# Value products a round later, the exponential's scale inside the minimum, and an early stage re-ordered

## The chip, the cores and the metric

The kernel runs on one NeuronCore of a Trainium2 chip. Five engines work from queues of their own and meet through semaphores: TensorE (PE in the profile, its weight loads PEld) multiplies matrices, VectorE (DVE) and ScalarE (ACT) do elementwise work and reductions, GpSimd (POOL) does smaller elementwise work, and SyncE (SP) issues the DMAs. The metric is the device time of one execution in microseconds (us).

## The reference

Two layers over a sequence of 2048 tokens of width 1024, each with eight input projections, two groups of heads and an output projection, and a residual around the whole. Cut to what matters:

```
hn = rms_norm(x, norm_gain)
aq, ak, av, ag, rq, rk, rv, rg = split(hn @ w_in)          # eight times 512 columns
# A: 8 heads of 64, chunks of 64 tokens, own chunk and 8 before it, learned bias by distance
p  = softmax(q k^T * 64**-0.5 + bias);  ya = p @ v
# B: 4 heads of 128, retention: decay by distance, rotary phases on q and k
t1*c - t2*s, t1*s + t2*c                                     # the rotation, halves of a head
yr = rms_norm(o_intra + o_inter)
y  = concat(ya * silu(ag), yr * silu(rg))
x  = x + y @ w_out
```

After the second layer comes a last RMSNorm. All in float32; the kernel keeps that precision by splitting each operand of a matmul into a high and a low half of 16 bits and adding three products (high by high, high by low, low by high).

## The kernel before

Activations lie transposed in `hTh` and `hTl` (high and low), in four blocks of 512 tokens for a layer. The loops run over layers `l`, over four groups of heads `s` (two attention heads and one retention head) and, inside, over the four token blocks `n`. For each (l, s, n) `dense_T` (L608) makes the four projections that are wanted transposed (attention q and k, retention q and k) as four PSUM tiles `dT` of 128 x 512, each with 24 matmuls of 512 columns (L731); `dense_V` (L738) makes the values and gates as four tiles `dV`, one for each 128 tokens, again 24 matmuls (L752). These tiles share two PSUM buffers (`psD`). ScalarE and VectorE evacuate them, in `evacuate` (L627) and, for `dV`, at L760 to L770.

The order of every engine but SP is written out by hand. `run` (L152) steps a dense generator, which yields after each third of a tile (8 matmuls): a *round*. In each round it fires what `later(k, fn)` (L595) had put off by k rounds, then steps the attention of the block before by one round, and then pulls some steps of background work (`push`, `pull`: weight preparation, norms, tables) so that it is spread over the rounds that are left. An engine works through its queue strictly in that order: an instruction that waits holds all that are behind it. SP's order is written out only for the first block, and is left to the scheduler after it.

`attention` (L778) handles eight units of a block (four tiles of 128 queries, `a`, by two heads, `hx`), three rounds each. In the first round it calls `flow(1)` (L588), which takes the oldest value product `pv` out of `pipe` if more than one is there, that of two units before; then `qk` puts the scores of this unit into PSUM tile `S` (L800, L801). VectorE adds the bias and takes the row maximum in one instruction (L804), makes the exponential's bias from it (L806), ScalarE takes the exponential (L807) and rounds it (L809), POOL makes the remainder (L810), and a transposing DMA on SP's queue (L812) brings both into `pT`, which has two buffers. `pv` multiplies `pT` by the values (L820 to L822) into a PSUM tile of its own for each head, from a ring of four (`psR`) that is shared with retention and with the column sums; `out_` (L824) takes the reciprocal of the row sum (L826), multiplies it by a scale (L827), and multiplies the head by it and by the gate (L832). Retention's products are made in `decayed` (L870) and `retention` (L884), in the units with hx = 1.

The rotation of retention's q and k (j = 2 and 3 in `evacuate`): ScalarE copies the tile to SBUF (L662), two DMAs swap the halves of the head (L666, L667), VectorE multiplies by cosine and sine tables and adds (L670), and the result is rounded and its remainder taken (L673, L676). The tables of a block come from `tables` (L83), some twenty small VectorE steps and two sines on ScalarE (L121, L122), stored to DRAM and loaded for each use (`tab_load`, L613).

Weights are loaded in sections of 128 columns; ScalarE sums their squares (`sumsq`, L305), VectorE casts the sum (`lowp`, L314), TensorE adds over partitions (`allsum`, L319), and the section is scaled by a power of two and split (`convert`). `prep_T` and `prep_V` do this for the next group, `prep_Omax` (L494) sums the squares of all of w_out.

The first block, (0, 0, 0), has an order of its own (the step list at L1363): its tokens are normalised and transposed tile by tile; tokens 512 to 1023 are normalised during its `dense_V`, one step of a list in each round (L1368), and `dense_T` of the second block needs them.

## Time and profile before

| | us |
|---|---|
| median of 3 runs | 2094.44 |
| lowest and highest | 2092.88, 2094.84 |
| the profiled execution | 2094.75 |
| its span | 2092.8 |

| engine | busy us | share of the span |
|---|---|---|
| PE | 2004.4 | 96% |
| VectorE | 1343.8 | 64% |
| ScalarE | 1141.3 | 55% |
| POOL | 432.9 | 21% |

The granted TensorE clock was 0.991 of full speed in the mean. A row of a group reads: line, engine, operation, tiles written and read, shapes, count, then busy time in us and the mean in ns of one instruction, then the idle time of the engine just ahead of them and what ended it. A row of waits reads: who waited for whom, total us, number of times, longest. A row of the timeline reads: start, duration, engine, line, instruction; in brackets the idle time ahead of it and what ended it.

### The profile page before, as it was taken

What the parts mean: (1) busy time and instruction counts of PE and PEld (TensorE: products, weight loads), DVE (VectorE), ACT (ScalarE), POOL (GpSimd) and SP (SyncE); (2) the same over time, 40 slices, a digit from 0 to 9 for tenths busy, and PEclk for the clock granted to TensorE, in tenths of its full rate; (3) what the DMA queues carried; (4) which work ended last, traced back from release to release, by engine and by line L of the source; (5) the groups of instructions that cost most, each with busy time, mean ns of one, the idle gap of its engine ahead of it and who ended that gap; (6) DMA issues with size and microseconds to landing.
All of it is one profiled execution on the core that took longest, in us unless ns stands there. A gap on an engine that the chain in (4) does not pass through costs nothing.

```text
span 2092.8 us, 39599 instructions
## 1 busy us (share of the span) xinstructions
PE 2004.4 (96%) x14014; PEld 1049.4 (50%) x14014; DVE 1343.8 (64%) x4031; ACT 1141.3 (55%) x2522; POOL 432.9 (21%) x509
## 2 busy tenths in 40 slices
PE   6888999999999999998999999999999999998998
PEld 4344455555555555444444555555555555554443
DVE  7676666666656666576654666666666667656643
ACT  7455665556565654455444546554655565455432
POOL 1022222222122212121000222222222222222100
PEclk9999999999999999999999999999999999999999
DMA  8767674557476764599965556655655776558874
GB/s 247 171 127 162 136 166 114 115 112 159 110 169 133 161 166 99 113 211 260 219 185 113 120 102 142 130 121 106 155 123 118 178 156 162 117 100 183 212 199 123
DMA packets 645702, 313.65 MB, mean 150 GB/s; under 512 B 459232, under 2 KB 602080, under 8 KB 645504
## 3 DMA queue, kind: packets, MB, share of 16 engines
q1 hardware_dynamic: 645504, 311.12, 66.4%
q8 instruction: 110, 1.80, 0.4%
q14 instruction: 88, 0.72, 0.1%
HBM read 123.26 MB, written 41.98 MB: 79 GB/s over the span
## 4 chain that ended last, share of the span: by engine, by line
PE 55%; DMA 7%; DVE 5%; ACT 3%; issue 1%; SPq 1%; POOL 0%; POOLq 0%; DVEq 0%; ACTq 0%
PE dT L731 18%; PE dV L752 15%; PE dO L1105 12%; DMA pT<-pq 2%; PE r L860 2%; PE S L801 2%; PE S L800 2%; PE o L820 1%; PE o L821 1%; PE o L822 1%; DVE sc L804 1%; DMA swp<-rot 1%; DMA yhy<-rhy 1%; ACT sc L807 1%; ACT pq L809 1%
## 5 line engine op out<-in xcount | busy, mean ns | idle before, releaser
L810 POOL TENSOR_TENSOR pq<-sc,pq 128x640 f16<-128x640 f32 (+4 forms) x256 | 323.8, 1265 | 1175.9 <-issue 590.7
L807 ACT ACTIVATE sc<-sc,mq,cT 128x640 f32<-128x640 f32 (+4 forms) x256 | 218.5, 853 | 558.1 <-DVE mq L806 413.7
L752 PE MATMUL dV<-whV,hTh 128*128 128x512 f16 x1024 | 354.5, 382 | 13.0 <-DVE gt L770 12.8
L731 PE MATMUL dT<-hTh,whT 128*128 128x512 f16 x1008 | 349.4, 382 | 14.7 <-DMA hTh<-hTl 9.6
L752 PE MATMUL dV<-wlV,hTh 128*128 128x512 f16 x1024 | 354.1, 381 | 0.0
L752 PE MATMUL dV<-whV,hTl 128*128 128x512 f16 x1024 | 354.0, 381 | 0.0
L731 PE MATMUL dT<-hTl,whT 128*128 128x512 f16 x1008 | 346.6, 379 | 0.0
L731 PE MATMUL dT<-hTh,wlT 128*128 128x512 f16 x1008 | 346.6, 379 | 0.0
L752 PEld LDWEIGHTS <-hTh 128*128 128x128 f16 x2048 | 197.3, 98 | 227.7 <-DVE gt L770 16.4
L731 PEld LDWEIGHTS <-whT 128*128 128x128 f16 x2016 | 192.9, 98 | 221.6 <-issue 24.1
L804 DVE CUSTOM_DVE_ANT_0 sc<-S,bias 128x640 f32<-128x640 f32 (+4 forms) x256 | 188.4, 736 | 78.8 <-PE S L801 61.1
L1105 PE MATMUL dO<-whO,yly 128*128 128x512 f16 x512 | 194.1, 379 | 2.4 <-DMA yly<-rly 2.4
L1105 PE MATMUL dO<-whO,yhy 128*128 128x512 f16 x512 | 194.0, 379 | 1.2 <-DVE gt L770 0.6
L1105 PE MATMUL dO<-wlO,yhy 128*128 128x512 f16 x512 | 194.0, 379 | 0.0
L809 ACT ACTIVATE pq<-sc 128x640 f16<-128x640 f32 (+4 forms) x256 | 171.5, 670 | 10.9 <-DMA pT<-pq 3.0
L1105 PEld LDWEIGHTS <-yhy 128*128 128x128 f16 x1024 | 99.6, 98 | 115.1 <-issue 0.8
L752 PEld LDWEIGHTS <-hTl 128*128 128x128 f16 x1024 | 99.7, 98 | 105.0 <-issue 2.8
L800 PE MATMUL S<-k,q 128*128 128x128 f16 (+3 forms) x592 | 143.1, 268 | 7.9 <-DVE mq L804 7.9
L731 PEld LDWEIGHTS <-wlT 128*128 128x128 f16 x1008 | 97.2, 98 | 101.8 <-issue 1.1
L820 PE MATMUL o<-v,pT 128*128 128x65 f16 x1120 | 129.6, 193 | 10.2 <-DMA pT<-pq 9.7
L801 PE MATMUL S<-k,q 128*128 128x128 f16 (+3 forms) x592 | 130.5, 268 | 0.0
L820 PEld LDWEIGHTS <-pT 128*128 128x128 f16 x1120 | 105.3, 97 | 49.2 <-DMA pT<-pq 21.3
(350 smaller groups left out, 3352.7 us busy)
## 6 DMA issues: line engine op xcount, KB each, us to landing
q<-qq SPq DMA_DIRECT2D x128, 128.0 KB, 2.7
yyy<-y_d SPq DMA_DIRECT2D x32, 512.0 KB, 4.6
stT<-in_w_in_dram SPq DMA_DIRECT2D x27, 512.0 KB, 4.8
stV<-in_w_in_dram SPq DMA_DIRECT2D x26, 512.0 KB, 4.5
k<-kk SPq DMA_DIRECT2D x128, 64.0 KB, 2.0
swp<-rot SPq DMA_DIRECT2D x64, 128.0 KB, 2.5
tabc<-tab SPq DMA_DIRECT2D x32, 256.0 KB, 2.7
tabs<-tab SPq DMA_DIRECT2D x32, 256.0 KB, 2.9
```

Of the source, the lines that this page charges most:

```text
L731: pe.matmul(ps, w_[:, j, kt, :], h_[:, kt, :], start=(m == 0), stop=(m == 23))
L752: pe.matmul(ps, h_[:, kt, a * P:(a + 1) * P], w_[:, kt, :], start=(m == 0), stop=(m == 23))
L800: pe.matmul(o, st.q[:, hx, 0, cs], k_, start=True, stop=False)
L801: pe.matmul(o, st.q[:, hx, 1, cs], k_, start=False, stop=True)
L804: dve.tensor_tensor_reduce(out=v, in0=S[:, 0:w], in1=g.bias[hx][:, 640 - w:640], scale=1.0, scalar=-3.0e38, op0=ALU.add, op1=ALU.max, accu ...
L807: act.activation(v, v, AF.Exp, bias=m[:, 0:1], scale=g.c[:, 0:1])
L809: act.activation(pq[:, 0:w], v, AF.Copy)
L810: pool.tensor_tensor(pq[:, w:2 * w], v, pq[:, 0:w], op=ALU.subtract)
L820: pe.matmul(o[:, 0:65], u.p[:, b, :], v_[:, 0:65], start=(b == 0), stop=False)
L821: pe.matmul(o[:, 0:64], u.p[:, b, :], v_[:, 65:129], start=False, stop=False)
L860: pe.matmul(out_, w_, m_, start=(i == 0), stop=(i + 1 == len(pairs)))
L1105: pe.matmul(ps, h_[:, kt, :], w_[:, kt, :], start=(m == 0), stop=(m == 23))
```

## The change

- `attention`: `flow(1)` is called after the unit's first round instead of ahead of its scores, so each value product stands one round later.
- `qk`: VectorE's instruction multiplies by the (negative) scale `g.nc`, read from a column, and takes the minimum; a POOL addition of one column replaces VectorE's L806, and the exponential's scale is -1.
- `pv` and `out_`: both heads of a query tile share one PSUM tile; after the second, one reciprocal and one multiplication serve two columns.
- `tables`: one round more ahead of the two sines, except for the first block.
- First block: the rotation reads the PSUM tile directly (VectorE multiplies by the sine with input and output on different halves of the partitions, in two instructions for a tile) instead of a ScalarE copy and two swap DMAs for each of the two tiles. Its first retention product is put 11 rounds after the start of its `dense_V` instead of into the attention.
- Second block: q and k of the attention are projected in eight pieces of 128 columns, with 24 matmuls each, in an order that takes the last 128 tokens last.
- Weight sums: the cast stands one round after ScalarE's sum of squares, in `prep_T` and `prep_V`; `prep_Omax` writes its eight sums into eight columns, reduces them once, loads two sections ahead, and is pushed one dense generator earlier with 22 steps.

```
@@ tables
         yield
+        if n:
+            yield
         act.activation(r, ang, AF.Sin)
         act.activation(k2, k, AF.Sin)
...
@@ Sections, prep_T
         def square(self, j):
             nm = f"{self.nm}{j}"
-            self.sq[j] = lowp(sumsq(self.sts[j], nm, self.g.h[:, j]), nm)
+            self.sq[j] = sumsq(self.sts[j], nm, self.g.h[:, j])
+
+        def cast(self, j):
+            self.sq[j] = lowp(self.sq[j], f"{self.nm}{j}")
...
             w.square(j)
             yield
+            w.cast(j)
             yield
...
@@ prep_Omax
+        load(0)
+        load(1)
+        yield
         for j in range(KT):
...
+            if j + 2 < KT:
+                load(j + 2)
+            yield
+            act.activation(st[j], st[j], AF.Square, accum_out=ms[:, j:j + 1])
+            yield
+        yield
+        m1 = b2.tile([P, 1], F32, tag="m1", name=f"m1{nm}", bufs=4)
+        dve.tensor_reduce(m1, ms, axis=AX.X, op=ALU.add)
+        mm = lowp(m1, nm)
+        for _ in range(2):
             yield
...
@@ dense_T
+        def first_rotation(j, ps, rot):
...
+            def cosine():
+                dve.scalar_tensor_tensor(out=own, in0=ps, scalar=2.0 ** -16, in1=st.tabc, op0=ALU.mult, op1=ALU.mult)
+
+            def sine(half):
...
+                i_, o_ = slice((1 - half) * 64, (2 - half) * 64), slice(half * 64, half * 64 + 64)
+                dve.scalar_tensor_tensor(out=st.swp[o_], in0=ps[i_], scalar=-2.0 ** -16, in1=st.tabs[i_], op0=ALU.mult,
+                                         op1=ALU.mult)
...
+            d = 2 * j
+            later(d, cosine)
+            later(d, lambda: sine(0))
+            later(d + 1, lambda: sine(1))
+            later(d + 2, lambda: dve.tensor_tensor(own, own, st.swp, op=ALU.add))
+            later(d + 3, lambda: act.activation(rot[:, 0], own, AF.Copy))
+            later(d + 4, lambda: dve.tensor_tensor(rot[:, 1], own, rot[:, 0], op=ALU.subtract))
...
+        parts = (l, s, n) == (0, 0, 1)
+        if parts:
+            ps, m = [None] * 2, 0
+            for (j, a) in ((0, 0), (0, 1), (0, 2), (1, 0), (1, 1), (1, 2), (0, 3), (1, 3)):
...
+                for i in range(24):
+                    w_, h_ = ((g.h, hh), (g.l, hh), (g.h, hl))[i // KT]
+                    pe.matmul(ps[j][:, cs], w_[:, j, i % KT, :], h_[:, i % KT, cs], start=(i == 0), stop=(i == 23))
...
@@ attention
-            dve.tensor_tensor_reduce(out=v, in0=S[:, 0:w], in1=g.bias[hx][:, 640 - w:640], scale=1.0, scalar=-3.0e38,
-                                     op0=ALU.add, op1=ALU.max, accum_out=m)
-            dve.tensor_scalar(m, m, g.nc[:, 0:1], LN_PSC, op0=ALU.mult, op1=ALU.add)
-            act.activation(v, v, AF.Exp, bias=m[:, 0:1], scale=g.c[:, 0:1])
+            dve.tensor_tensor_reduce(out=v, in0=S[:, 0:w], in1=g.bias[hx][:, 640 - w:640], scale=g.nc[:, 0:1],
+                                     scalar=3.0e38, op0=ALU.add, op1=ALU.min, accum_out=m)
+            pool.tensor_tensor(m, m, lnp, op=ALU.add)
+            act.activation(v, v, AF.Exp, bias=m[:, 0:1], scale=-1.0)
...
+                rl = b2.tile([P, 2], F32, tag="rl", name=f"rl{u.nm}")
+                dve.reciprocal(rl, o2[:, 0:2, 64])
+                dve.tensor_scalar(rl, rl, g.ka[:, 0:1], None, op0=ALU.mult)
...
         for i, (a, hx) in enumerate(units):
+            u = qk(a, hx)
+            yield
             flow(1)
-            u = qk(a, hx)
-            yield
...
-            elif a == 0 and (l, s, n) == (0, 0, 0):
-                decayed(l, s, n, g, st, 0)
...
@@ the loop over blocks
+                if n == 2 and s == 2:
+                    push(prep_Omax(l, go), 22)
...
-                if n == 2 and s == 2:
-                    push(prep_Omax(l, go), 13)
...
-                if (n, s) == (0, 0) and not first:
+                if (n, s) == (0, 0):
                     later(11, lambda n=n, g=g, st=st: decayed(l, s, n, g, st, 0))
```

More of the change, by code (lines that the diff above doesn't have):

```diff
@@ L62, in hybrid_trunk @@
     pool.memset(mhalf, -0.5)
+    lnp = cp.tile([P, 1], F32, tag="lnp", name="lnp")
+    pool.memset(lnp, LN_PSC)
     invf_sb = cp.tile([P, 1], F32, tag="invf", name="invf_sb")
@@ L134, in tables @@
         yield
-    TAB_STEPS = 19
+    TAB_STEPS = 20
     class St:
@@ L441, in prep_V @@
             yield
-            m1[j] = lowp(sq(j), f"{nm}{j}")
-            yield from rest(3)
+            m1[j] = sq(j)
+            yield
+            m1[j] = lowp(m1[j], f"{nm}{j}")
+            yield from rest(2)
             m = allsum(m1[j], f"{nm}{j}")
@@ L495, in prep_Omax, with load @@
         nm = f"O{l}"
-        mm = b2.tile([P, 1], F32, tag="omax", name=f"omax{nm}")
-        st = load_sec(w_out[l, :, 0:P], f"{nm}m0")
+        ms = b2.tile([P, KT], F32, tag="omax", name=f"omax{nm}", bufs=1)
+        st = []
+        def load(j):
+            t_ = w4.tile([P, KT, P], F32, tag="w4", name=f"st{nm}m{j}")
+            sp.dma_start(t_, w_out[l, :, j * P:(j + 1) * P].rearrange("(k p) c -> p k c", p=P))
+            st.append(t_)
+        load(0)
+        load(1)
+        yield
         for j in range(KT):
+            if j + 2 < KT:
+                load(j + 2)
             yield
-            m1 = sumsq(st, f"{nm}m{j}", None)
-            if j + 1 < KT:
-                st = load_sec(w_out[l, :, (j + 1) * P:(j + 2) * P], f"{nm}m{j + 1}")
-            if j == 0:
-                dve.tensor_copy(mm, m1)
-            else:
-                dve.tensor_tensor(mm, mm, m1, op=ALU.add)
-        mm = lowp(mm, nm)
-        for _ in range(4):
+            act.activation(st[j], st[j], AF.Square, accum_out=ms[:, j:j + 1])
[5 more added lines that the diff above has]
+        for _ in range(2):
             yield
@@ L625, in soon, with tokens @@
                 later(1, fn)
+        def first_rotation(j, ps, rot):
+            if j == 2:
+                st.rq = rot
+                later(1, tab_load)
+                own = rot[:, 1:3].rearrange("p a c -> p (a c)").bitcast(F32)
+            else:
+                st.rk = rot
+                own = b1.tile([P, 512], F32, tag="qq", name=f"raw{nm}")
+            st.swp = []
+            def cosine():
+                dve.scalar_tensor_tensor(out=own, in0=ps, scalar=2.0 ** -16, in1=st.tabc, op0=ALU.mult, op1=ALU.mult)
+            def sine(half):
+                if half == 0:
+                    st.swp = b1.tile([P, 512], F32, tag="swp", name=f"swp{nm}_{j}")
+                i_, o_ = slice((1 - half) * 64, (2 - half) * 64), slice(half * 64, half * 64 + 64)
+                dve.scalar_tensor_tensor(out=st.swp[o_], in0=ps[i_], scalar=-2.0 ** -16, in1=st.tabs[i_], op0=ALU.mult,
+                                         op1=ALU.mult)
+            def tokens():
+                st.kt = b1.tile([P, KT, P], F16, tag="ktok", name=f"kt{nm}")
+                sp.dma_start_transpose(out=st.kt, in_=rot.rearrange("p a c -> p (a c)"))
+            d = 2 * j
[5 more added lines that the diff above has]
+            later(d + 4, lambda: dve.tensor_tensor(rot[:, 1], own, rot[:, 0], op=ALU.subtract))
+            if j == 2:
+                later(d + 5, lambda: act.activation(rot[:, 2], rot[:, 0], AF.Copy, scale=2.0 ** -11))
+            else:
+                later(d + 6, tokens)
         def evacuate(j, ps):
@@ L657, in evacuate @@
                 rot = b2.tile([P, w, 512], F16, tag=f"rot{j}", name=f"rot{nm}_{j}")
+                if first:
+                    first_rotation(j, ps, rot)
+                    return
                 if j == 2:
@@ L683, in tokens @@
                         sp.dma_start_transpose(out=st.kt, in_=rot.rearrange("p a c -> p (a c)"))
-                    d = 5 if j == 2 and first else 3
+                    d = 3
                     later(d, turned(raw, raw, st.tabc, ALU.mult))
@@ L693, in swap @@
                     else:
-                        later(d + 5 if first else 11, tokens)
+                        later(11, tokens)
                 if j == 2:
@@ L698, in evacuate @@
                     swap()
-                    if first:
-                        later(1, tab_load)
                 else:
                     st.rk = rot
-                    later(8 if first else 2, swap)
+                    later(2, swap)
         if first:
@@ L717, in dense_T @@
                 yield
-        for j in range(2 if first else 0, 4):
+        parts = (l, s, n) == (0, 0, 1)
+        if parts:
+            ps, m = [None] * 2, 0
+            for (j, a) in ((0, 0), (0, 1), (0, 2), (1, 0), (1, 1), (1, 2), (0, 3), (1, 3)):
+                if a == 0:
+                    ps[j] = psD.tile([P, 512], F32, tag="dense", name=f"dT{nm}_{j}")
+                cs = slice(a * P, (a + 1) * P)
+                for i in range(24):
+                    w_, h_ = ((g.h, hh), (g.l, hh), (g.h, hl))[i // KT]
+                    pe.matmul(ps[j][:, cs], w_[:, j, i % KT, :], h_[:, i % KT, cs], start=(i == 0), stop=(i == 23))
+                    m += 1
+                    if m % 32 == 0 and m < 192:
+                        yield
+                if a == 3:
+                    evacuate(j, ps[j])
+            yield
+        for j in range(2 if first or parts else 0, 4):
             if j == 2 and not first:
@@ L782, in attention @@
                 units.append((a, hx))
-        ya = {}
         def qk(a, hx):
@@ L816, in pv @@
             t = 4 * n + u.a
-            o = psR.tile([P, 512], F32, tag="small", name=f"o{u.nm}")
+            if u.hx == 0:
+                ring["o"] = psR.tile([P, 4, P], F32, tag="small", name=f"o{u.nm}")
+            o2 = ring["o"]
+            o = o2[:, u.hx]
             for b, (q_, a_) in enumerate(u.kts):
@@ L822, in pv @@
                 pe.matmul(o[:, 0:65], u.p[:, u.nb + b, :], v_[:, 0:65], start=False, stop=(b == u.nb - 1))
+            if u.hx == 0:
+                return
             def out_():
-                rl = b2.tile([P, 1], F32, tag="rl", name=f"rl{u.nm}")
-                dve.reciprocal(rl, o[:, 64:65])
-                dve.tensor_tensor(rl, rl, g.ka, op=ALU.mult)
-                if u.hx == 0:
-                    ya[u.a] = b2.tile([P, P], F32, tag="ya", name=f"ya{u.nm}")
-                y = ya[u.a]
-                vs = slice(u.hx * 64, u.hx * 64 + 64)
-                dve.scalar_tensor_tensor(out=y[:, vs], in0=o[:, 0:64], scalar=rl[:, 0:1], in1=st.g[u.a][:, vs],
-                                         op0=ALU.mult, op1=ALU.mult)
-                if u.hx == 1:
-                    sp.dma_start(y_d[t][:, s * P:(s + 1) * P], y)
+                rl = b2.tile([P, 2], F32, tag="rl", name=f"rl{u.nm}")
+                dve.reciprocal(rl, o2[:, 0:2, 64])
+                dve.tensor_scalar(rl, rl, g.ka[:, 0:1], None, op0=ALU.mult)
+                y = b2.tile([P, P], F32, tag="ya", name=f"ya{u.nm}")
+                for hx in range(2):
+                    vs = slice(hx * 64, hx * 64 + 64)
+                    dve.scalar_tensor_tensor(out=y[:, vs], in0=o2[:, hx, 0:64], scalar=rl[:, hx:hx + 1],
+                                             in1=st.g[u.a][:, vs], op0=ALU.mult, op1=ALU.mult)
+                sp.dma_start(y_d[t][:, s * P:(s + 1) * P], y)
             later(1, out_)
@@ L840, in attention @@
         for i, (a, hx) in enumerate(units):
-            flow(1)
             u = qk(a, hx)
             yield
+            flow(1)
             if hx == 1:
```

## The prediction

> **What bounds the kernel now.** I read the page's first lines, then the table by stage, then TensorE's waits, then the timeline around the longest.

> ```profile
> span 2092.8 us, 39599 instructions
> PE 2004.4 (96%) x14014; PEld 1049.4 (50%) x14014; DVE 1343.8 (64%) x4031; ACT 1141.3 (55%) x2522; POOL 432.9 (21%) x509
> ```

> TensorE (PE) is the bound: 88 us of the span are left to it in which it does nothing. A change that adds and removes no matmul work can only win from those 88 us, and from matmuls run at a reduced clock. Where they lie, by stage (columns: stretch and its length, then busy time of PE, weight loads, VectorE, ScalarE and POOL, then granted clock, DMA share, GB/s):

> ```profile
> 69.00:205.00 136.00, 107.26 (x693) 54.11 (x692) 95.50 (x269) 72.69 (x154) 26.57 (x35) 0.92 0.71 150
> 205.00:860.00 655.00, 644.29 (x4793) 343.39 (x4793) 425.19 (x1378) 375.89 (x874) 157.18 (x176) 1.00 0.64 136
> 860.00:985.00 125.00, 112.13 (x767) 56.69 (x766) 82.29 (x231) 69.03 (x132) 24.82 (x26) 0.97 0.92 207
> 1090.00:1870.00 780.00, 776.06 (x5636) 411.04 (x5635) 503.42 (x1573) 435.00 (x1025) 180.36 (x204) 1.00 0.60 131
> ```

> The long steady stretches leave TensorE 11 us idle in 655 and 4 us in 780. The early stretch, 69 to 205 us, leaves 29 of 136 and runs at 0.92 of the clock; the hand-over between layers leaves 13 of 125, with the DMA engines 92% busy. What TensorE waits for:

> ```profile
> PE dV L752 <- DVE gt L770: 12.8, 6, 4.9
> PE o L820 <- DMA pT<-pq: 9.7, 11, 2.2
> PE dT L731 <- DMA hTh<-hTl: 9.6, 1, 9.6
> PE msT L323 <- DVE mbT L316: 3.3, 3, 1.9
> PE msV L323 <- DVE ya L832: 2.9, 2, 1.6
> ```

> **Step A, first rotation from PSUM and the second block's projection in parts.** The stake:

> ```profile
> 78.91 3.26 PE L731 MATMUL dT<-hTh,whT 128*128 128x512 f16 x8 [9.64 <-DMA hTh<-hTl]
> 82.00 0.22 PE L800 MATMUL S<-k,q 128*128 128x128 f16 x1
> 82.11 1.89 PE L731 MATMUL dT<-hTh,wlT 128*128 128x512 f16 x8
> 78.11 0.69 DVE L670 TENSOR_TENSOR raw<-raw,tabc 128x512 f32<-128x512 f32 x1 [7.20 <-DMA swp<-raw]
> 72.41 0.59 SPq L667 DMA_DIRECT2D swp<-raw  x1
> 73.10 1.53 SPq L236 DMA_TRANSPOSE hTh<-hTl  x1
> ```

> At full clock a 512-column matmul takes (1.89 - 0.38) / 7 = 0.216 us. The eight after the wait took 3.09 us where 1.73 would do, so the stake is 9.6 + 1.4 = 11.0 us. The change takes four swap DMAs off SP's queue; two of them (0.59 us the one shown) stand just ahead of the last token tile's transposes, and VectorE's 7.20 us behind that DMA goes too. The parts let six of eight column pieces start before the last token tile has landed. Their price:

> ```profile
> 33.44 0.61 PE L712 MATMUL dT<-hTl,whT 128*128 128x128 f16 x8
> 33.89 0.61 PE L712 MATMUL dT<-hTh,wlT 128*128 128x128 f16 x8
> 69.58 1.34 DVE L93 SCALAR_TENSOR_TENSOR xa<-xa 128x256 f32<-128x256 f32 x3
> ```

> 192 matmuls of 128 columns at 0.45 / 8 = 0.056 us are 10.7 us, against 48 x 0.216 = 10.4: +0.3. What is late next is VectorE. Four operations (about 0.69 us each) of the second rotated tile move ahead of 70 us, and the sine product is now two instructions for each tile, as an instruction on half the partitions takes as long: 6 x 0.69 = 4.1 us more before 70 us, in a queue that also holds the token tiles' remainders that TensorE waits for. VectorE was through with its list at 69.58 + 1.34 = 70.9, so it would be through at about 73 to 75. The first retention product is now put into TensorE's order 11 rounds into the value projection, ahead of that projection's last eight matmuls, so at 78.91 - 9.64 - 1.7 = 67.6 us, and needs the last of that rotation. If it waits until 73, TensorE then does 8 matmuls (1.7), the parts (10.7), some 0.5 of attention products and 1.4 for a low clock, and is through at 87.3; before, it was through at 82.1 + 40 x 0.216 + 0.5 = 91.2. That is a gain of 4. If nothing waits it is 11; if the new table products wait for the table's DMA as well, it is -2. I take 6, nearer to the 4, for which the queue speaks.

> **Step B, sines a round later.**

> ```profile
> 129.54 0.61 PE L752 MATMUL dV<-whV,hTh 128*128 128x512 f16 x1 [4.88 <-DVE gt L770]
> 129.94 0.63 PE L752 MATMUL dV<-whV,hTl 128*128 128x512 f16 x1
> 192.54 0.61 PE L752 MATMUL dV<-whV,hTh 128*128 128x512 f16 x1 [4.25 <-DVE gt L770]
> 124.36 1.28 ACT L121 ACT_TABLE_LOAD   x1
> 126.28 0.26 ACT L760 ACTIVATE v<-dV 128x128 f16<-128x128 f32 x1
> 126.54 1.28 ACT L761 ACT_TABLE_LOAD   x1
> 140.13 1.89 PE L731 MATMUL dT<-hTh,whT 128*128 128x512 f16 x8 [2.21 <-issue]
> 204.90 1.44 PE L731 MATMUL dT<-hTh,whT 128*128 128x512 f16 x3 [2.81 <-DMA hTh<-rhn]
> ```

> The two waits for a PSUM buffer stand behind an evacuation (L760) that came after the sines: 126.28 - 124.36 = 1.9 us, and the table load back, 1.3. A round later they stand behind that evacuation. Each wait shrinks by 3.2 us, and the eight matmuls after it, 0.43 instead of 0.216 us apart, give back 1.7: 4.9 each, 9.8 for both. But the sines still run on ScalarE before the last tokens of the next block are rounded, and TensorE already stood 2.21 and 2.81 us at the start of the next block, the second time for those tokens. Arriving earlier, it waits there longer. Between 0 and 9.8 I take 4.

> [...]

> **Step C, value products a round later.** They gain about a round against the landing of the transposed weights, at least 8 x 0.216 = 1.7 us, and all eleven waits are 2.2 us or shorter: up to 9.7 us. The buffers of pT are two, so the transpose of unit i must now wait for the products of unit i-2, which have moved behind unit i's scores. They end one round after the scores; the source is ready later:

> ```profile
> 142.23 0.38 PE L800 MATMUL S<-k,q 128*128 128x512 f16 x1
> 144.09 0.92 ACT L807 ACTIVATE sc<-sc,mq,cT 128x640 f32<-128x640 f32 x1 [2.85 <-DVE mq L806]
> 145.85 1.40 POOL L810 TENSOR_TENSOR pq<-sc,pq 128x640 f16<-128x640 f32 x1 [4.82 <-ACT pq L809]
> ```

> that is 147.25 - 142.23 = 5.0 us after them. So nothing is lost there. Against the gain stands the slower minimum (step E), and the hand-over stretch with its 0.92 DMA share, where a wait on the next transfer may follow. Bounds 0 and 9.7; I take 6.

> **Step D, sums of squares apart from VectorE, and w_out's sum of squares rewritten.**

> ```profile
> DVE mbT L316 <- ACT whT L309: 36.7, 24, 2.5
> PE r L860 <- DVE dT L868: 1.1, 1, 1.1
> PE msO L323 <- DVE yr L925: 0.7, 1, 0.7
> ```

> VectorE stood 36.7 us in front of the cast that now comes a round later, with retention and evacuation work queued behind it. TensorE's share is the 3.3 us of msT and, at w_out's sums, 1.8 us in layer 0 (the last two rows, 620 to 642 us) and as much again in layer 1: 6.9. The 2.9 of msV wait for a PSUM buffer that head output still holds; heads sharing a tile hold it longer and take half as many, so I leave it. The cast is nearer to its matmul by a round, w_out's by two; bounds 0 and 9.8, I take 5.

> **Step E, scale in the minimum, heads divided at once.**

> ```profile
> L806 DVE TENSOR_SCALAR mq<-mq,ncT 128x1 f32<-128x1 f32 x256 | 54.8, 214 | 9.1
> L826 DVE RECIPROCAL rl<-o 128x1 f32<-128x1 f32 x256 | 40.9, 160 | 0.0
> L827 DVE TENSOR_TENSOR rl<-rl,kaV 128x1 f32<-128x1 f32 x256 | 59.7, 233 | 8.9
> L212 POOL TENSOR_TENSOR rsn<-ssn,mhalf 128x1 f32<-128x1 f32 x32 | 18.2, 572 | 194.8 <-DVE ssn L210 194.8
> 100.80 1.22 DVE L231 TENSOR_TENSOR rln<-hTh,rhn 128x1024 f16<-128x1024 f32 x1
> 100.96 1.67 POOL L921 TENSOR_TENSOR rss<-rss,mhalf 128x1 f32<-128x1 f32 x1 [3.57 <-DVE rss L920]
> ```

> VectorE loses 54.8 + 40.9 / 2 + 59.7 / 2 = 105 us, of an engine that is 64% busy: worth 0 beside TensorE, at most the 2.9 us of msV. POOL gets 256 additions of one column; the nearest row is 0.57 us where VectorE took 0.21, and 1.67 beside a long VectorE operation. So the exponential starts 0.35 to 1.5 us later in each unit. Its cover is the round gained in C for the weights, and for ScalarE's evacuations the time of a whole projection tile (24 x 0.216 = 5.2 us) before its buffer is wanted. I take 0; if 0.15 us a unit came through, it would be 38 us. The reduction now reads its scale from a column; no row has that, and I take it as equal.

> **Sum**, against the profiled execution (2094.75 us, 1.95 outside its span, 0.3 above the median 2094.44): 6 + 4 + 6 + 5 + 0 = 21, so 2073.8 us.

> **Rivals.** (1) New waits take over: TensorE arrives early and stands for tokens in A and B (2 and 0 left of 10), C gives 3, D gives 5: 2084.8. The 2.21 and 2.81 us speak for it; VectorE's 70% (95.5 of 136) in that stretch, which falls, speaks against. (2) Slower: POOL in the chain of the exponential. From 21 / 256 = 0.08 us a unit on TensorE's path it eats the whole gain; at 0.15 us the time is 2094.75 - 21 + 38 = 2112. For it: the 1.67 us row. Against it: the steady stretches have hardly a wait on ScalarE's chain. [...] (3) The value products' shift does nothing, since the transposes move with them: 2079.8; the 5.0 us above speak against it.

> **How the numbers follow.** Forecast (gain of 12 to 33 us, its own range 2062 to 2083) 0.50; rival 1 with rival 3 (gain of 4.2 to 12) 0.22; more than that gained 0.04; within 0.2% (4.2 us, about what a measurement of this kernel can tell from no change) 0.08; rival 2 0.16. Faster 0.76, same 0.08, slower 0.16. The range 2060 to 2098 leaves out 0.04 below and most of rival 2, 0.14, above.

> **What would show it.** In the profile after: the 9.64 us wait gone and at most some 6 us at the first retention product or the parts; waits for gt at 1 us; TensorE's waits for pT under 4 us in total; msT and the waits near w_out's sums gone; the stretch from 69 to 205 us shorter by some 10 us. Wrong if the wait on hTh<-rhn grows by what the sines gave, or ScalarE's wait before the exponential rises above 0.15 us a unit in TensorE's idle time.

## The result and the profile after

The changed kernel takes 2106.8 us (median; 2105.7 to 2109.3) against 2094.6 for the kernel before on the same chip: a ratio of 1.0058, 95% interval 1.0046 to 1.0071. It is 0.6% slower; 2073.8 was predicted. Its profiled execution took 2109.25 us, the longest of its four and 2.4 above the median. The first lines of the page:

```profile
span 2107.5 us, 39606 instructions
...
PE 2013.4 (96%) x14158; PEld 1060.7 (50%) x14158; DVE 1273.5 (60%) x3507; ACT 1115.6 (53%) x2520; POOL 524.5 (25%) x766
```

The span grew by 14.7 us. TensorE's idle time grew from 88.4 to 2107.5 - 2013.4 = 94.1 us, only 5.7; its busy time grew by 9.0, of which the parts of the second block's projection explain 0.3 by the prediction's own working. (What is said of profiles here and below compares one execution of each kernel.) VectorE lost 70 us of work and GpSimd (POOL) gained 92. TensorE's waits in the changed kernel (engine, line, what released it: us in total, times, longest):

```profile
PE dV L824 <- DVE gt L842: 15.0, 8, 3.5
PE S L871 <- DVE mq L875: 14.6, 11, 2.8
PE msT L327 <- DVE mbT L320: 12.4, 11, 2.3
PE dT L803 <- DMA hTh<-rhn: 8.5, 2, 5.0
...
PE msO L327 <- DVE mbO L320: 3.6, 2, 1.8
...
PE o L894 <- DMA pT<-pq: 3.0, 2, 2.2
```

The 9.6 us wait for the last token tile is gone, and the waits for transposed weights (pT) fell from 9.7 to 3.0, as forecast. What was to fall and did not are the waits for gt (12.8 before) and for mbT (3.3 before); the wait for a score buffer (S) is up from 7.9, that for tokens (hTh) from 2.8.

Most of the added busy time is a matter of the clock: summed over the stretches that a trace shows at half clock, the busy time lost to it is 11.7 us before and 18.0 after, 6.3 of the 9.0. The stretch from the third to the fourth block of layer 0, from one block's first value evacuation to the next one's, in the table by stretch of the kernel before and then of the changed kernel (length, busy time of PE, weight loads, VectorE, ScalarE and POOL with their instructions, then granted clock, DMA share, GB/s):

```profile
177.06:244.50 67.44, 54.62 (x384) 28.24 (x383) 42.84 (x129) 40.88 (x86) 15.14 (x16) 0.92 0.71 155
```

```profile
177.68:249.75 72.07, 59.70 (x380) 29.41 (x378) 39.20 (x116) 40.16 (x86) 21.06 (x24) 0.86 0.62 143
```

It is 4.6 us longer, the largest step that the next block doesn't give back, with as many matmuls within four: the granted clock fell from 0.92 to 0.86, and TensorE was busy 5.1 us longer on the same work. Waits of TensorE in the changed kernel up to the end of that stretch, from its timeline (start, us, engine, line, operation, and in brackets the wait ahead of it). Not all of them brought the clock down: the single matmuls at 67.87 and 125.71 still took 0.39 us, the one at 194.00 took 0.61:

```profile
67.87 0.39 PE L824 MATMUL dV<-whV,hTh 128*128 128x512 f16 x1 [3.27 <-DVE gt L842]
...
74.01 0.23 PE L932 MATMUL r<-rot,rot 128*128 128x128 f16 x1 [2.02 <-DVE rot L676]
...
125.71 0.39 PE L824 MATMUL dV<-whV,hTh 128*128 128x512 f16 x1 [1.92 <-DVE gt L842]
...
137.48 3.57 PE L803 MATMUL dT<-hTh,whT 128*128 128x512 f16 x8 [5.03 <-DMA hTh<-rhn]
...
194.00 0.61 PE L824 MATMUL dV<-whV,hTh 128*128 128x512 f16 x1 [3.46 <-DVE gt L842]
...
207.27 3.57 PE L803 MATMUL dT<-hTh,whT 128*128 128x512 f16 x8 [3.48 <-DMA hTh<-rhn]
...
232.95 0.16 PE L327 MATMUL msT<-mbT,ones 128*128 128x1 bf16 x1 [2.31 <-DVE mbT L320]
```

How such a wait comes about, from the timeline ahead of the last of these rows:

```profile
227.57 1.28 DVE L337 SCALAR_TENSOR_TENSOR wlT<-stT,sT,whT 128x1024 f16<-128x1024 f32 x1
227.79 1.11 POOL L877 TENSOR_TENSOR mq<-mq,lnp 128x1 f32<-128x1 f32 x1 [3.48 <-DMA k<-kk]
...
228.94 0.83 ACT L878 ACTIVATE sc<-sc,mq 128x640 f32<-128x640 f32 x1 [1.24 <-POOL mq L877]
...
231.58 1.04 ACT L313 ACTIVATE whT<-stT 128x1024 f16<-128x1024 f32 x1
...
232.74 0.16 DVE L320 CAST mbT<-m1T 128x1 bf16<-128x1 f32 x1 [1.41 <-ACT whT L313]
```

ScalarE stood 1.24 us for GpSimd's addition, then worked without a pause up to the sum of squares at 231.58; VectorE's cast waited for that sum, and TensorE's matmul for the cast.

The suspect is the new addition on GpSimd, between minimum and exponential. All its 256 instructions, from the answer for its line (duration in ns, least/median/most), and two of them in the timeline:

```profile
L877 POOL TENSOR_TENSOR mq<-mq,lnp x256: 184/192/1171, 80.2 to 1973.4; 128x1 f32<-128x1 f32 x128
```

```profile
236.92 0.89 DVE L875 CUSTOM_DVE_ANT_0 sc<-S,bias,ncT 128x640 f32<-128x640 f32 x1 [2.62 <-PE S L872]
...
237.72 1.28 DVE L337 SCALAR_TENSOR_TENSOR wlT<-stT,sT,whT 128x1024 f16<-128x1024 f32 x1
237.95 1.10 POOL L877 TENSOR_TENSOR mq<-mq,lnp 128x1 f32<-128x1 f32 x1 [4.05 <-DVE mq L875]
...
239.09 0.83 ACT L878 ACTIVATE sc<-sc,mq 128x640 f32<-128x640 f32 x1 [4.13 <-POOL mq L877]
...
1202.05 0.88 DVE L875 CUSTOM_DVE_ANT_0 sc<-S,bias,ncT 128x640 f32<-128x640 f32 x1 [0.62 <-PE S L872]
...
1203.08 0.19 POOL L877 TENSOR_TENSOR mq<-mq,lnp 128x1 f32<-128x1 f32 x1 [1.73 <-DVE mq L875]
1203.31 0.83 ACT L878 ACTIVATE sc<-sc,mq 128x640 f32<-128x640 f32 x1 [2.63 <-POOL mq L877]
```

At 1203 the addition takes 0.19 us and the exponential starts 0.38 us behind the minimum (1202.05 + 0.88 to 1203.31). At 238 VectorE went straight on to an operation with two operands in SBUF; the addition took 1.10 us, to the end of that operation, and the exponential started 1.28 us behind. Of the 256 additions 79 took over 0.35 us, each of them beside a VectorE operation on two SBUF tiles.

### The profile page after: what moved, and what is told of

Read it like the earlier page. It is cut to its first block, busy times and chain, and to the rows that moved or that the text cites. A ratio compares the mean times of both kernels' runs of the same rounds, so it can differ in the third digit from the quotient of the medians.

```text
span 2107.5 us, 39606 instructions
## 1 busy us (share of the span) xinstructions
PE 2013.4 (96%) x14158; PEld 1060.7 (50%) x14158; DVE 1273.5 (60%) x3507; ACT 1115.6 (53%) x2520; POOL 524.5 (25%) x766
## 3 DMA queue, kind: packets, MB, share of 16 engines
q8 instruction: 111, 1.82, 0.4%
## 5 line engine op out<-in xcount | busy, mean ns | idle before, releaser
L878 ACT ACTIVATE sc<-sc,mq 128x640 f32<-128x640 f32 (+4 forms) x256 | 194.9, 761 | 574.4 <-POOL mq L877 574.4
L803 PE MATMUL dT<-hTl,whT 128*128 128x512 f16 x992 | 342.1, 379 | 0.0
L803 PEld LDWEIGHTS <-whT 128*128 128x128 f16 x1984 | 188.1, 98 | 200.1 <-issue 16.0
L877 POOL TENSOR_TENSOR mq<-mq,lnp 128x1 f32<-128x1 f32 x256 | 93.5, 365 | 715.9 <-DVE mq L875 601.3
L875 DVE CUSTOM_DVE_ANT_0 sc<-S,bias,ncT 128x640 f32<-128x640 f32 (+4 forms) x256 | 203.1, 793 | 54.8 <-PE S L872 44.1
L1177 PE MATMUL dO<-whO,yhy 128*128 128x512 f16 x512 | 194.8, 380 | 2.4 <-DVE gt L842 1.5
L940 DVE SCALAR_TENSOR_TENSOR sh<-sh,state 128x128 f16<-128x128 f16 x120 | 102.8, 857 | 118.8 <-ACT sh L936 118.8
L871 PE MATMUL S<-k,q 128*128 128x128 f16 (+3 forms) x592 | 144.4, 270 | 15.8 <-DVE mq L875 14.6
```

What stands on the lines that cost most here:

```text
L803: pe.matmul(ps, w_[:, j, kt, :], h_[:, kt, :], start=(m == 0), stop=(m == 23))
L871: pe.matmul(o, st.q[:, hx, 0, cs], k_, start=True, stop=False)
L875: dve.tensor_tensor_reduce(out=v, in0=S[:, 0:w], in1=g.bias[hx][:, 640 - w:640], scale=g.nc[:, 0:1], scalar=3.0e38, op0=ALU.add, op1=ALU.m ...
L877: pool.tensor_tensor(m, m, lnp, op=ALU.add)
L878: act.activation(v, v, AF.Exp, bias=m[:, 0:1], scale=-1.0)
L940: dve.scalar_tensor_tensor(out=dst[:, 1], in0=dst[:, 0], scalar=-2.0 ** 11, in1=src, op0=ALU.mult, op1=ALU.add)
```

## The experiments

Each kernel was timed beside the kernel before on the same chip. The medians of the latter differ a little from chip to chip (2094.5 to 2096.5), so the ratios are what is compared. "Delay" is the mean over the 256 units of a trace, from the end of the minimum (of the maximum in the kernel before) to the start of the exponential.

| kernel | us | ratio, 95% interval | delay, us |
|---|---|---|---|
| before | 2094.6 | 1 | 0.351 |
| minimum's part alone, as changed (GpSimd) | 2105.6 | 1.0043 (1.0031 to 1.0056) | 0.542 |
| the same, addition on VectorE | 2089.7 | 0.9973 (0.9962 to 0.9984) | 0.291 |
| the same, no addition | 2082.9 | 0.9937 (0.9925 to 0.9949) | 0.108 |
| changed kernel (GpSimd) | 2106.8 | 1.0058 (1.0046 to 1.0071) | 0.549 |
| changed, addition on ScalarE | 2096.0 | 1.0004 (0.9996 to 1.0013) | 0.449 |
| changed, addition on VectorE | 2085.2 | 0.9963 (0.9950 to 0.9975) | 0.306 |
| changed, no addition | 2078.7 | 0.9919 (0.9905 to 0.9933) | 0.106 |

**The parts one by one.** The first four runs made one part each, the last of them the two that belong to the early blocks. Value products a round later, alone:

```diff
-            flow(1)
             u = qk(a, hx)
             yield
+            flow(1)
```

> The kernel before with one part alone: the value products a round later. By the prediction's step C it gains 6 us (0 to 9.7), with the 9.7 us of waits for pT nearly gone. By the rival (SyncE's queue: with two buffers of pT each transpose now stands in that queue until the value products of two units before are done, and the transfers behind it are late) the waits for pT go as well, but SyncE waits on TensorE for some 50 us more, VectorE waits longer for the swapped halves (31.7 us before, 88.5 in the changed kernel), and the time is 2 to 6 us longer than before.

Measured: 2101.6 us, 1.0026 (1.0016 to 1.0035). Slower by 5.4 us. TensorE's waits in it, and one of VectorE's:

```profile
PE r L860 <- DVE ya L832: 4.1, 4, 2.8
PE msT L323 <- DVE ya L832: 3.6, 6, 0.9
PE o L820 <- DMA pT<-pq: 3.5, 3, 2.3
```

```profile
DVE rot L670 <- DMA swp<-rot: 78.9, 29, 5.6
```

The waits for pT fell to 3.5, as forecast. New are 7.7 us for buffers of the small PSUM ring, released by a later evacuation of the value products (ya), and VectorE stands 78.9 us for the rotary's half swaps, against 31.7. The rival's time holds.

The minimum's part alone:

```diff
-            dve.tensor_tensor_reduce(..., scale=1.0, scalar=-3.0e38, op0=ALU.add, op1=ALU.max, accum_out=m)
-            dve.tensor_scalar(m, m, g.nc[:, 0:1], LN_PSC, op0=ALU.mult, op1=ALU.add)
-            act.activation(v, v, AF.Exp, bias=m[:, 0:1], scale=g.c[:, 0:1])
+            dve.tensor_tensor_reduce(..., scale=g.nc[:, 0:1], scalar=3.0e38, op0=ALU.add, op1=ALU.min, accum_out=m)
+            pool.tensor_tensor(m, m, lnp, op=ALU.add)
+            act.activation(v, v, AF.Exp, bias=m[:, 0:1], scale=-1.0)
```

> The kernel before with one part alone: scale in the minimum, the addition on POOL. By the prediction's step E nothing (-1 to +1 us). By its rival 2 slower: ScalarE's exponential starts later, VectorE waits longer for what ScalarE makes behind it (45 us before for the state's upper half, 119 in the changed kernel), and the time is 4 us longer or more.

Measured: 2105.6, 1.0043: 9 us, three quarters of the loss of 12, in one part.

The cast of the weights' squares a round later, alone (the same in the two other places that cast such a sum):

```diff
             w.square(j)
             yield
+            w.cast(j)
             yield
```

> The kernel before with one part alone: the cast of the weights' sums a round later. By the prediction's step D it gains about 3 us, TensorE's 3.3 us of waits for the sums gone. By the rival (the cast stands behind a further round of VectorE's queue, two rounds ahead of the matmul that needs it instead of three) TensorE's waits for the sums grow from 3.3 to 9 us or more and the time is 5 to 9 us longer.

Measured: 2098.8, 1.0013 (1.0001 to 1.0025). The waits it was to take away grew (msT from 3.3 to 7.7 us); the loss, 2.7 us, is half of what the rival gave at the least.

The first block's part: rotation from PSUM with the first retention product moved, and the second block's projection in parts:

```diff
+                if first:
+                    first_rotation(j, ps, rot)
+                    return
...
-        for j in range(2 if first else 0, 4):
+        parts = (l, s, n) == (0, 0, 1)
...
+        for j in range(2 if first or parts else 0, 4):
```

> The kernel before with two parts alone: the first rotation from PSUM (with its first retention product moved) and the second block's projection in parts. By the prediction's step A it gains 6 us (-2 to 11). By the prediction's rival 1 the 9.6 us wait goes, but a later wait of TensorE for the next block's tokens (2.2 and 2.8 us before) grows by as much, and the time is within 2 us of before.

Measured: 2095.7, 0.9997 (0.9987 to 1.0007). At the second block's first value evacuation this kernel was 4.9 us ahead of the kernel before, still 1.7 at that of layer 0's last block, and 1.4 behind at the end of its span, in one trace each. The time is what rival 1 gave, but not by its mechanism: the next blocks did not take the gain back (5.4 us at layer 0's last block of the first group), and it was lost much later, 3 us of it from the twelfth to the fourteenth of layer 0's sixteen blocks. By which waits is not shown.

**What it is in the minimum's part.** Two things had changed there: GpSimd in the chain, and the scale that VectorE reads from a column (877 ns for the 640-wide form against 819).

```diff
-            pool.tensor_tensor(m, m, lnp, op=ALU.add)
+            dve.tensor_scalar(m, m, LN_PSC, None, op0=ALU.add)
```

> The scale column stays in the minimum and the exponential keeps its immediate scale, but the addition of the logarithm goes back to VectorE (256 x one 128x1 operation, as before the change). Theory 1, GpSimd in the chain: its addition took 192 ns when nothing else ran and 0.5 to 1.2 us in 78 of 256 units, each beside a VectorE operation with two operands in SBUF; with it gone the +9 us of the minimum's part alone go too: 2094 to 2098, ratio 0.999 to 1.001. Theory 2, the scale column (877 ns against 819 for the 640-wide form): the time stays at 2102 to 2106.

Measured: 2089.7. Not only is the loss gone, it is 0.27% faster than the kernel before, more than theory 1 gave. The scale column is paid back in the exponential, whose median fell from 920 to 828 ns with an immediate scale (the answers for its line, of the kernel before and of this one):

```profile
L807 ACT ACTIVATE sc<-sc,mq,cT x256: 492/920/924, 83.4 to 1958.6; 128x640 f32<-128x640 f32 x96, 128x128 f32<-128x128 f32 x8, 128x256 f32<-128x256 f32 x8, 128x384 f32<-128x384 f32 x8
```

```profile
L807 ACT ACTIVATE sc<-sc,mq x256: 401/828/832, 82.3 to 1953.9; 128x640 f32<-128x640 f32 x96, 128x128 f32<-128x128 f32 x8, 128x256 f32<-128x256 f32 x8, 128x384 f32<-128x384 f32 x8
```

Then the line of the addition taken out:

> As the run with the addition on VectorE, but the addition is left out altogether (the probabilities are not scaled by 1024 ahead of their split into two halves). Theory 1 (GpSimd in the chain): the exponential starts right behind the minimum, nothing is lost: 2091 to 2097. Theory 2 (scale column): 2101 to 2105, since the 58 ns a unit are still ahead of the exponential.

Measured: 2082.9, 0.63% faster than before, better than either theory expected. With the part around it unchanged, a longer delay goes with a longer time: 0.108, 0.291 and 0.542 us give 2082.9, 2089.7 and 2105.6.

The same in the whole kernel, addition on VectorE:

> The changed kernel with one edit: the addition of the logarithm on VectorE in place of GpSimd. Theory (GpSimd's addition, held up by VectorE's operations, is most of the loss): the 16 us that lie between the minimum's part with the addition on GpSimd (2105.6) and on VectorE (2089.7) come off, 2089 to 2094. Rival (several parts each cost, the addition is only one): no more than 5 us come off, 2101 to 2106.

Measured: 2085.2, 0.9963. So the place of the addition, GpSimd in place of VectorE, costs the changed kernel about 20 us (1.0058 - 0.9963 of 2095), more than the 16 of the theory, and with VectorE's addition the change gains 0.37%. First lines and waits of this kernel:

```profile
span 2083.1 us, 39492 instructions
...
PE 2005.5 (96%) x14158; PEld 1057.3 (51%) x14158; DVE 1308.9 (63%) x3763; ACT 1118.5 (54%) x2520; POOL 432.7 (21%) x509
```

```profile
PE dV L824 <- DVE gt L842: 14.4, 7, 4.7
PE S L871 <- DVE mq L875: 10.8, 8, 2.7
PE dT L803 <- DMA hTh<-rhn: 8.7, 2, 4.9
...
PE msT L325 <- DVE mbT L318: 3.4, 6, 1.3
PE msO L325 <- DVE mbO L318: 2.9, 2, 1.5
...
PE o L894 <- DMA pT<-pq: 2.3, 2, 2.1
```

Of the 24.4 us between the two spans 7.9 are busy time (5.4 of them by the clock, summed as above) and 16.5 idle. The row that grew most is msT, 12.4 against 3.4: the matmul of the timeline above. The next is the score buffer, 14.6 against 10.8.

Is it GpSimd, or any separate step? The addition on ScalarE:

```diff
-            pool.tensor_tensor(m, m, lnp, op=ALU.add)
+            act.activation(m, m, AF.Identity, bias=lnp[:, 0:1])
```

> The changed kernel with the addition on ScalarE, just ahead of the exponential, in place of GpSimd: the same operation, one semaphore less, and no engine that VectorE's operations hold up. Theory (GpSimd's addition is held up by VectorE's two-operand operations, 78 of 256 lengthened from 0.19 to as much as 1.2 us, and costs two hand-overs): 2084 to 2091, as with the addition on VectorE. Rival (any addition outside VectorE between minimum and exponential costs, since it stands in the queue of a busy engine): 2096 to 2107.

> The changed kernel without the addition (the probabilities are not scaled by 1024). Theory (what counts is the time from a unit's scores to its exponential): another 4 to 9 us below the changed kernel with the addition on VectorE (2085.2), as it was 6.9 without the other parts: 2076 to 2081. Rival (with value products a round later that time is hidden): 2083 to 2086.

Measured: 2096.0 and 2078.7. ScalarE's addition (294 ns, the median) comes out at the lower edge of the rival: it costs 9 us more than VectorE's, and GpSimd's 11 more than ScalarE's. So GpSimd is not needed for a loss, and in the four kernels the order of the times is that of the delays. The times do not grow in proportion (by the ratios the first 0.20 us of delay cost 9 us, the next 0.14 another 9, the last 0.10 then 11), and the addition also loads the engine that makes it, 75 us in all on ScalarE; the runs do not part the two. That VectorE lengthens GpSimd's delay is shown: by the median delay (0.378 us), what the long cases add to the mean is 0.17 of the 0.24 us by which it exceeds VectorE's.

**Parts that cost alone and not in company.** Two more parts alone, both heads' reciprocals and evacuations at once, and `prep_Omax` rewritten:

```diff
-            o = psR.tile([P, 512], F32, tag="small", name=f"o{u.nm}")
+            if u.hx == 0:
+                ring["o"] = psR.tile([P, 4, P], F32, tag="small", name=f"o{u.nm}")
...
-                dve.reciprocal(rl, o[:, 64:65])
+                dve.reciprocal(rl, o2[:, 0:2, 64])
```

```diff
-            m1 = sumsq(st, f"{nm}m{j}", None)
...
-                dve.tensor_tensor(mm, mm, m1, op=ALU.add)
+            act.activation(st[j], st[j], AF.Square, accum_out=ms[:, j:j + 1])
...
+        dve.tensor_reduce(m1, ms, axis=AX.X, op=ALU.add)
...
-                    push(prep_Omax(l, go), 13)
+                    push(prep_Omax(l, go), 22)
```

The expectations of the latter, here and below, word it loosely: the squares run on ScalarE in both kernels; what differs is that VectorE adds them once at the end, that two sections are loaded ahead, and when and in how many steps it runs.

> Only the heads divided together. Theory: VectorE waits some 20 us for the second head's products at its reciprocal, which lies off the path; 2094 to 2097, ratio 0.999 to 1.001. Rival: the evacuation, a head later, is what the retention products and the transposes now wait for (r<-ya, new waits of TensorE): 2098 to 2101.

> Only the squares of the output weights on ScalarE and their start a round block later. Theory: the two blocks in which it now runs are about 5 us longer each and the ones after it 3 us shorter, as in the changed kernel, so +3 to +5 us: 2098 to 2100. Rival (the prediction's): the 3.6 us of waits at the maximum go, 2091 to 2094.

Measured: heads 2104.0, 1.0036 (1.0022 to 1.0050); w_out's squares 2099.4, 1.0014 (1.0006 to 1.0023). The heads cost 7.5 us, more than either theory gave, and not in the waits that the rival named; the waits for pT are the largest now and those for gt follow:

```profile
PE o L822 <- DMA pT<-pq: 14.6, 15, 2.0
PE dV L752 <- DVE gt L770: 13.4, 9, 4.9
```

With the addition on VectorE, value products and heads were put back in the whole, one at a time:

> The changed kernel with the addition on VectorE and the value products where they were before the change. Theory 1, value products a round later cost in any company (5.4 us alone): 2078 to 2082. Theory 2, they pay once the heads are divided together and the others are in: 2088 to 2095.

> The changed kernel with the addition on VectorE and each head divided by itself, as before the change. Theory 1, dividing heads together costs in any company (7.5 us alone): 2076 to 2081. Theory 2, its cost alone came from the value products standing a round earlier, so that VectorE waited for the second head; with them later nothing changes or it gains: 2084 to 2092.

Measured: values early 2093.6, 0.9991 (0.9982 to 1.0000); heads apart 2091.9, 0.9977 (0.9966 to 0.9988). So in company the later value products gain 0.28%, where alone they lost 0.26; the heads together, which alone lost 0.36%, lose nothing (0.9963 against 0.9977, the intervals just overlap). One row of each bears on how they may need each other, values early first:

```profile
PE o L894 <- DMA pT<-pq: 9.0, 10, 2.3
```

```profile
PE r L930 <- DVE ya L904: 4.0, 4, 2.7
```

Heads together without later values leave the products waiting for their weights (14.6 and 9.0 us in the two kernels, 9.7 in the kernel before). Later values without heads together leave the small PSUM ring waiting for evacuations (4.1 and 4.0 us on the retention product). With both, the first is 2.3 and the second isn't among the waits. That one tile of the ring for two heads is what pays for holding it longer would fit, but it is argued, not shown: the difference is more than these waits, no run has the two parts without the others, and none has the whole with both put back.

`prep_Omax` put back in the whole, with VectorE's addition and without any:

> The changed kernel with the addition on VectorE and the output weights' squares as before the change (on VectorE, a round block earlier). Theory (the squares on ScalarE delay the exponentials of the two blocks in which they run, 3 us each, of which the next block gives back all): within 2 us of 2085.2. Rival (2.9 us, as alone): 2081 to 2083.

> The same without the addition (the probabilities are not scaled by 1024). Theory: as the changed kernel without it, 2078.7 within 2 us. Rival: 2075 to 2077, faster than every kernel so far.

Measured: 2087.1, 0.9959 (0.9945 to 0.9972), no difference from 0.9963; and 2074.8, 0.9899 (0.9884 to 0.9915), the fastest kernel of the study, 1.0% below the kernel before, though its interval overlaps that of the changed kernel without the addition (0.9919). In company the rewritten squares cost nothing that can be told.

**SyncE's queue.** In the kernel with later values alone, a unit's transpose waited 42.6 us in SyncE's queue for the products to free its buffer, with the swaps behind it. To take that away, the swaps were issued from ScalarE's queue, with and without later values:

```diff
-                    sp.dma_start(swp[0:64, :], raw[64:128, :])
-                    sp.dma_start(swp[64:128, :], raw[0:64, :])
+                    act.dma_start(swp[0:64, :], raw[64:128, :])
+                    act.dma_start(swp[64:128, :], raw[0:64, :])
```

> Value products a round later (alone 2101.6), and the rotary's two half swaps issued from ScalarE's queue, which has just written what they read, in place of SyncE's. Theory, SyncE's queue: the transpose of a unit now waits in SyncE's queue for a buffer that the later value products free (43 waits, 42.6 us), and the swaps wait behind it; VectorE's wait for the swaps (78.9 us against 31.7) falls to 35 us or less and the time to 2095 to 2098. Rival, later outputs: TensorE's and VectorE's order with the later evacuation costs the 5 us by itself; VectorE's wait for the swaps falls too, but the time stays at 2100 to 2103.

> The control: the kernel before with only the swaps on ScalarE's queue. Theory: 128 issues on ScalarE cost nothing that TensorE sees and the 31.7 us of VectorE's waits shrink somewhat, 2093 to 2097. Rival: the issues delay ScalarE's exponentials, 2098 to 2102.

Measured: 2101.5, 1.0035 (1.0021 to 1.0048), and for the control 2112.0, 1.0083 (1.0070 to 1.0097). The theory's sign is missing: VectorE's wait for the swaps is 69.3 us, not 35 or less. The control costs 17 us by itself, more than either theory gave. Beside it, the later value products gain 0.48% (10 us), where on the kernel before they lost 0.26%; TensorE's waits for pT, of the control and of the pair:

```profile
PE o L820 <- DMA pT<-pq: 14.3, 14, 2.5
```

```profile
PE o L820 <- DMA pT<-pq: 4.4, 3, 2.1
```

So the later products can gain with each head divided by itself, though the retention product still waits 4.0 us for the ring, and the heads' shared tile is not the only company in which they pay. Why is open. The two waits of the theory are as long or longer in another kernel, the changed one with VectorE's addition, and it is 9 us faster than the kernel before:

```profile
DVE rot L726 <- DMA swp<-rot: 78.2, 29, 6.7
```

```profile
SPq L883 <- PE o L896: 64.3, 60, 2.0
```

So such waits do not by themselves make a kernel slower.

**Does the first block's gain stay?** The first block's part with the minimum's part and no addition:

> The minimum with the scale and no addition at all (alone 2082.9; the probabilities are not scaled by 1024), with the first block's rotation from PSUM and the second block's projection in parts (alone 2095.7, no change). Theory: the early gain of 5 us was given back because VectorE and the exponential chain were late in later blocks; with that chain 0.2 us shorter a unit some of it stays: 2077 to 2082. Rival: the parts don't add, 2082 to 2086.

Measured: 2079.7, 0.9933 (0.9921 to 0.9946), against 0.9937 without the first block's part. In us that lies in the theory's range, but the kernel before was 2 us faster on this chip, and by the ratios nothing that can be told is added, as the rival had it. In one trace each, 2.4 us more were gained by the second block (3.2 against 0.8), and they were gone at the end (11.4 against 11.7).

## Why the prediction was wrong, step by step

**Step E is the one that failed.** It saw that "the exponential starts 0.35 to 1.5 us later in each unit", and took 0 because of a cover: the round gained in step C, and a projection tile's time for ScalarE's evacuations. Measured, the delay grew by 0.20 us in the mean over the kernel before, and by 0.24 over VectorE's addition, and the latter cost about 20 us. The cover was argued for the weights and the evacuations alone, and for these it held: the waits for pT are 3.0 us against 2.3 with VectorE's addition, those for gt 15.0 against 14.4. What paid was the rest of ScalarE's queue, above all the sums of squares for the next weights (msT, 9.0 of the 16.5 us of idle time), and the clock. Rival 2 named this mechanism: 20 / 256 = 0.08 us a unit, a third of the 0.24, came through to TensorE, close to the 21 / 256 at which it has the whole gain eaten. The 1.67 us row, which spoke for that rival, has its like in this trace: an addition took 1.10 us beside VectorE's 1.28 (at 237.95), and 0.19 in the median of the 177 that are not among the 79 long ones. The scale from a column, taken as equal, costs 58 ns in the 640-wide form, and the exponential gave back 92; that was a gain left out. With VectorE's addition this part alone gains 0.27%, some 6 us that the sum does not have.

**Without the addition on GpSimd the gain is 9, not 21.** The other steps were sized too high as well. That 2085.2 is close to rival 1's 2084.8 is luck: its 10 us are 2, 0, 3 and 5 for steps A to D, and the runs show no gain that lasts for A and none for D, waits that were taken back for B, and some 6 us each for C and for the minimum's part.

Step A (6): the 9.6 us wait went, VectorE was late next as forecast (2.02 us at the first retention product, 3.27 for gt ahead of it), and the gain of 4.9 us at the second block is close to the 6. But alone it came to nothing at the end of the kernel. The step ended its account at 91 us of 2093.

Step B (4): the waits for gt at 129.54 and 192.54, 4.88 and 4.25 us, are 1.92 and 3.46 now, and the waits at the next block's start, 2.21 and 2.81, are 5.03 and 3.48. 14.2 us before, 13.9 after: the tokens took it back, which was its lower bound and the first half of rival 1. The sines weren't run alone.

Step C (6): the waits for pT fell to 3.0, under the 4 that were named. "So nothing is lost there" was wrong: alone, the transposes stood 42.6 us in SyncE's queue for the products, where they stood for none before, and TensorE 7.7 us for the small PSUM ring, which the step did not look at; which of these made the loss is not shown. In the company of the other parts it gains 0.28% (5.9 us), close to the 6; alone it loses as much. Rival 3 is refuted, since the waits did fall; its chance stood in the wrong place, too, as its 2079.8 is a gain of 15 and not of 4.2 to 12.

Step D (5): 0 or less. Both halves cost alone (2.7 and 2.9 us), and w_out's made no difference in the whole; there, with VectorE's addition, msT's waits stand at 3.4 us, where they were 3.3, and those of msO at 2.9. The wait of VectorE in front of the cast, 36.7 us, did shrink, to 8.9, and no gain of TensorE's from it is seen.

The heads at once, half of step E, "worth 0": alone they cost 7.5 us, in company nothing that can be told.

## What to carry to other kernels

Price an instruction that is put into a chain by the delay it makes in that chain first, and not by the share of time for which the engine that takes it is busy: here VectorE, 64% busy, was the better place than GpSimd, 21% busy, by 20 us, and leaving the instruction out was better still, though the probabilities are then not scaled. A cover must be shown for everything queued behind the late instruction on its engine. And parts of a change that share a buffer ring are to be run in company as well as apart: two parts that lost 5 and 7 us alone gained 6 and lost nothing beside the other parts.

## What had not been expected of the hardware

The length of a single wait does not say whether the clock falls. In the kernel before, TensorE waited 1.94 us at 180.89 and 0.53 at 181.86, and the stretch kept its full clock; in the changed kernel it waited 1.88 at 181.52 and 0.53 at 182.49, and the same stretch ran at 0.79:

```profile
180.00:188.00 8.00, 6.58 (x50) 3.47 (x49) 7.86 (x20) 4.76 (x7) 1.95 (x2) 1.00 0.49 97
```

```profile
180.00:188.00 8.00, 5.95 (x27) 2.64 (x27) 6.43 (x17) 3.68 (x5) 2.01 (x3) 0.79 0.52 97
```

Two rows of the prediction's step B look like a limit between 2.21 and 2.81 us: after the wait of 2.21, at 140.13, eight matmuls of 512 columns took 1.89 us, 0.216 apart; after that of 2.81, at 204.90, three took 1.44, 0.42 apart. The traces show none that holds for a single wait: in the changed kernel the matmul after 3.27 us, at 67.87, took 0.39.

```profile
177.29:180.70 3.41, 1.67 (x11) 0.84 (x10) 2.45 (x5) 2.04 (x6) 0.89 (x2) 1.00 1.02 162
180.70:184.12 3.42, 2.70 (x28) 1.58 (x28) 3.35 (x12) 0.60 (x1) 0.55 (x1) 1.00 0.62 129
```

```profile
179.15:182.56 3.41, 1.00 (x12) 0.60 (x10) 3.38 (x10) 1.69 (x2) 0.55 (x1) 1.00 0.65 102
```

Before, the waits fell into two steps, in which TensorE was idle 1.74 and 0.72 us; after, into one, 2.41 us, and the next step ran at half clock. In these traces it is the idle time of a whole step that counts, however many waits it is made of: from 60 us on to 20 us ahead of the end, of the steps at full clock in all twenty traces every one with more than 2.02 us of idle time was followed by half clock (138), and none with less than 1.88. In the kernel before six were, of 2.13 to 3.41 us, and the others had 1.82 or less; in the changed kernel nine, of 2.13 to 2.77, and the others had 1.90 or less. So part of the clock's loss is luck, too: the same two waits cost 1.7 us in one trace (half of the 3.41 from 182.56 to 185.97, through which TensorE was busy at a clock of 0.50) and nothing in the other, by where the grid lay. No step had to be idle throughout: 2.41 us of 3.41 were enough.
